# Three projection chunks on rows times scale, shift by one-column products, and earlier operands at three later seams

## The chip, the cores and the metric

The kernel runs on one core of a Trainium2 chip. Five engines work from queues of their own, each in its own order: TensorE (PE, matrix products; its weight loads are listed apart as PEld), VectorE (DVE), ScalarE (ACT), GpSimd (POOL) and SyncE (SP, which here issues the DMA transfers). The metric is the device time of one execution in microseconds (us); lower is better. A run of this kernel has one core and therefore one time.

## The reference

Two layers of a decoder trunk on 1024 tokens of width 1024, batch 1, everything in fp32. Every sub-layer has the same frame:

```python
x = x + gate(c) * rmsnorm_post(f(rmsnorm_pre(x) * (1 + scale(c)) + shift(c)))
# scale, shift, gate: columns of silu(c) @ ada_w + ada_b   (1024 x 6144 weights for each layer)
# layer 0: f = [Mamba-2 SSD heads | MLA heads], read from one projection h @ w_in,
z, xbc, dt_raw, q_a, kv_a, k_pe = split_cols(h @ w_in, L0_SIZES)
xbc = silu(causal_depthwise_conv(xbc, conv_w, conv_b))       # four taps along the tokens
dt  = softplus(dt_raw + dt_bias)
#          then one output projection; then f = SwiGLU FFN with hidden width 2816
# layer 1: f = [GLA heads | NSA heads] in the same way, then its FFN
```

What matters here is the very first product of the program, `h @ w_in` of layer 0 with `h = rmsnorm(x) * gain * (1 + scale) + shift`. With `a = gain * (1 + scale)`, it is also `(rmsnorm(x) * a) @ w_in + shift @ w_in`, and the second term is one number for each column of `w_in`, the same for all tokens. The matrices of scale and shift must be summed from `ada_w` first: eight blocks of 128 rows and 1024 columns (512 KB) each.

## The kernel before

**Products.** An fp32 product is made of three products of a rounded type (`mm3`, L111): each operand is split into a high part (a ScalarE copy, L132 for weights, L144 for activations) and a low part (a subtraction, L133 and L145, mostly on VectorE), and TensorE makes high x high (L114), low x high (L115) and high x low (L116). A *chunk* is 128 columns of `l0_w_in` against all tokens, turned so that columns lie on the partitions. It comes in two *halves* of 512 tokens; a half is 8 blocks of the width times 3 products, 24 products into one PSUM bank. PSUM has the banks `bk` (4), `cx` (2) and `sm` (2). The activations `hT` lie in numbered `slab` tiles, four for each half of the tokens, two with high parts and two with low ones.

**Order.** The functions are written in the order of a list of work, and a scheduler gives each engine its own queue by the priority that follows from it. Transfers are issued by SyncE in the order of its queue, and an issue that must wait holds those behind it.

**The start** (`first_h`, L344). SyncE loads eight `ada_w` blocks for scale, then eight for shift (`aw`, five buffers), with rows of x between them. VectorE multiplies each block by a column of `silu(c)` and accumulates (L369, L371). Eight small products with a vector of ones turn the sum into columns (`ada_cols`, L286). Each of the eight x tiles (128 tokens) is squared and summed on ScalarE (L158), its reciprocal root comes from GpSimd (L151, L152), it is scaled by ScalarE (the first four, L353) or VectorE (the last four, L391), transposed by TensorE (L360) and copied into `xT` (L361). When shift is there, VectorE forms `xT*a + s` (L382), ScalarE takes the high part, and VectorE and GpSimd take turns with the low part.

**The first chunks** (`mixer0_ssd`, L599). Chunk 0 (k_pe and dt), with its chain for dt (L569 to L590: transposes, softplus, a triangular product), runs interleaved with chunks 6 and 7, the first two of twelve chunks `xbc`; then come the other ten, one at a time. A chunk of `xbc` is copied out of its bank by ScalarE, and its four-tap convolution and silu run on VectorE (L639, L641, L558) while TensorE is at the next chunks. Later come `z`, the latent chunks and the scan, whose first product (L751) reads the last convolutions back. Blocks of `ada_w` for the later sub-layers are accumulated beside all this (L276), one step at each `pump`.

**The entry of MLA** (`mixer0_latent`, then `mla`). The latent's last chunks end with `token_sumsq` (L848), 24 one-column products that give sums of squares per token; from them come `rstd` and `rq` (L877, VectorE). `mla` then splits `w_v` (a tile called `qt`, L132 and L133) and makes V.

**The FFN's output** (`ffn_out`) goes through 77 *jobs*. A job has an operand tile of two transfers (L1519, L1520), a high part (L1527) and a low part (L1528), and 12 products. Jobs 0 to 4 are prepared early, while the part before it runs; jobs 5 and up take their tiles from the pool `ab`, which is opened once the part before has closed its own. `front` (L1594) then forms the new x by rows, and in layer 0 also normalises them (L391, VectorE) for layer 1.

## Time and profile before

| | |
|---|---|
| three runs | 3165.64, 3176.91, 3178.05 us; median 3176.91 |
| the profiled execution | 3170.91 us, of which the span from first to last instruction is 3169.2 |
| mean granted TensorE clock in it | 0.982 of full |
| TensorE busy | 3015.1 us, 95% of the span |
| VectorE, ScalarE, GpSimd busy | 2166.4, 1313.2, 716.8 us |
| first product of a chunk | at 59.80 us |
| first product of the FFN's output | at 1264.74 us (layer 0) |

Times in the profile count from the start of the span. A row of the timeline has start, duration, engine (SPq is SyncE's queue), line, operation, output<-input, shape and count; behind it, in square brackets, stands how long the engine was idle before and who released it. A row of the stretches has the stretch, its length, then for PE, PEld, DVE, ACT and POOL the busy time and in brackets the count; then the granted clock of TensorE, the share of time that the DMA engines were busy, and GB/s. L12 is line 12 of the kernel before.

### The profile page before, as it was taken

The page shows a single profiled execution, that of the slowest core. Times are in us where ns is not written, and L with a number is a line of the kernel's source. Part 1 is how long each engine was busy: PE and PEld are TensorE (multiplying, and loading weights), DVE is VectorE, ACT ScalarE, POOL GpSimd, SP SyncE. Part 2 cuts the span into 40 slices and gives each one's busy share as a digit, 9 for nine tenths or more (in the row PEclk, how much of TensorE's full clock was granted, in tenths as well). Part 3 has the DMA queues.
Part 4 walks back from the last instruction along what each step waited for, and adds up shares of the span by engine and source line. Part 5 has one row for each costly group of instructions (what it writes and reads, how often), then busy time and mean ns, then how long its engine had stood idle before and what let it go on. Part 6 is the DMA issues. An engine that isn't in the chain of part 4 may idle for free. (4 is left out here: it accounts for less than half of the span.)

```text
span 3169.2 us, 42961 instructions
## 1 busy us (share of the span) xinstructions
PE 3015.1 (95%) x15832; PEld 2439.2 (77%) x15832; DVE 2166.4 (68%) x3375; ACT 1313.2 (41%) x2159; POOL 716.8 (23%) x678
## 2 busy tenths in 40 slices
PE   5999999999899999999999999889999999999998
PEld 4787777677787888787888888767777787888786
DVE  6667656767887777666737554677766877777655
ACT  4345334545632223445432432355555632223433
POOL 3003334210133223001204423022222114222001
PEclk9999989999999999999999999999999999999999
DMA  6555533324645455984425333331312645455854
GB/s 220 152 187 192 186 99 107 99 73 143 219 156 187 172 202 192 314 281 166 151 93 188 107 120 120 122 107 56 99 49 89 230 165 181 161 207 201 294 195 156
DMA packets 222866, 510.16 MB, mean 161 GB/s; under 512 B 23824, under 2 KB 62832, under 8 KB 221632
## 3 DMA queue, kind: packets, MB, share of 16 engines
q1 hardware_dynamic: 222656, 507.42, 47.0%
q8 instruction: 125, 2.05, 0.3%
q14 instruction: 85, 0.70, 0.1%
HBM read 370.09 MB, written 137.25 MB: 160 GB/s over the span
## 5 line engine op out<-in xcount | busy, mean ns | idle before, releaser
L115 PE MATMUL bk<-slab,whi 128*128 128x512 f32 x1208 | 479.5, 397 | 2.3 <-DVE slab L145 2.3
L114 PE MATMUL bk<-slab,whi 128*128 128x512 f32 x784 | 325.4, 415 | 6.7 <-ACT whi L132 3.5
L116 PE MATMUL bk<-slab,wlo 128*128 128x512 f32 x784 | 311.4, 397 | 2.4 <-DVE wlo L133 2.4
L115 PEld LDWEIGHTS bk<-slab,whi 128*128 128x128 f32 x1208 | 230.4, 191 | 53.3 <-DVE slab L145 3.2
L114 PE MATMUL bk<-T,whi 128*128 128x512 f32 x528 | 210.3, 398 | 2.5 <-DVE blk L1422 2.5
L116 PE MATMUL bk<-T,wlo 128*128 128x512 f32 x528 | 207.8, 394 | 0.0
L151 POOL TENSOR_SCALAR rstd<-ss 128x1 f32<-128x1 f32 (+1 forms) x86 | 31.7, 369 | 713.6 <-ACT junk L158 640.7
L114 PEld LDWEIGHTS bk<-slab,whi 128*128 128x128 f32 x784 | 151.3, 193 | 43.7 <-issue 7.0
L116 PEld LDWEIGHTS bk<-slab,wlo 128*128 128x128 f32 x784 | 150.1, 191 | 35.6 <-DVE wlo L133 2.6
L1218 ACT ACTIVATE whi<-rawa 128x512 fp32r<-128x512 f32 (+1 forms) x108 | 80.6, 749 | 190.0 <-PE bk L115 159.3
L114 PE MATMUL cx<-slab,whi 128*128 128x512 f32 x368 | 146.5, 399 | 6.6 <-ACT blk L1270 5.9
L2172 POOL TENSOR_SCALAR pexp<-pexp,rs 128x640 f32<-128x640 f32 (+7 forms) x128 | 96.3, 756 | 245.6 <-DVE rs L2171 95.2
L115 PE MATMUL cx<-slab,whi 128*128 128x512 f32 x368 | 145.2, 395 | 0.6 <-DVE slab L145 0.6
L116 PE MATMUL cx<-slab,wlo 128*128 128x512 f32 x368 | 145.3, 395 | 0.0
L1004 PE MATMUL sm<-ident,pexp 128*128 128x128 f32 x816 | 132.4, 278 | 6.2 <-POOL pexp L2172 2.3
L1446 POOL TENSOR_TENSOR blk<-blk,blk 128x512 f32<-128x512 f32 x22 | 35.3, 1604 | 423.9 <-DVE blk L1442 327.1
L1004 PEld LDWEIGHTS sm<-ident,pexp 128*128 128x128 f32 x816 | 93.5, 140 | 43.9 <-issue 19.6
L1006 ACT COPY pT<-sm 128x512 f32<-128x512 f32 (+2 forms) x144 | 76.4, 531 | 113.0 <-PE sm L1004 112.4
L1219 DVE TENSOR_TENSOR wlo<-rawa,whi 128x512 fp32r<-128x512 f32 (+1 forms) x108 | 118.2, 1095 | 7.2 <-ACT whi L1218 6.5
L114 PEld LDWEIGHTS bk<-T,whi 128*128 128x128 f32 x528 | 99.0, 188 | 28.1 <-DVE blk L1422 3.3
L276 DVE SCALAR_TENSOR_TENSOR adaacc<-ada,silu_c,adaacc 128x1024 f32<-128x1024 f32 x70 | 100.3, 1432 | 28.8 <-DMA ada<-in_l_ada_w_dram 28.6
L2168 ACT ACTIVATE pexp<-pexp,nm 128x640 f32<-128x640 f32 (+7 forms) x128 | 94.0, 735 | 60.8 <-DVE nm L2166 44.7
(635 smaller groups left out, 8505.9 us busy)
## 6 DMA issues: line engine op xcount, KB each, us to landing
ada<-in_l_ada_w_dram SPq DMA_DIRECT2D x80, 512.0 KB, 4.1
hid<-blk SPq DMA_DIRECT2D x154, 256.0 KB, 2.0
raw<-in_l_w_in_dram SPq DMA_DIRECT2D x51, 512.0 KB, 3.6
ab<-hid SPq DMA_DIRECT2D x96, 256.0 KB, 4.4
cat<-cat SPq DMA_DIRECT2D x64, 256.0 KB, 2.6
ab<-wt SPq DMA_DIRECT2D x60, 256.0 KB, 4.2
raw<-in_l_w_gate_dram SPq DMA_DIRECT2D x28, 512.0 KB, 3.6
raw<-in_l_w_up_dram SPq DMA_DIRECT2D x28, 512.0 KB, 4.5
```

The source lines that it names most:

```text
L114: mm(out, lh, rh, start=start, stop=False, skip_group_check=more)
L115: mm(out, lh, rl, start=False, stop=False, skip_group_check=more)
L116: mm(out, ll, rh, start=False, stop=stop, skip_group_check=more)
L151: nc.gpsimd.tensor_scalar(r, ss, inv_d, EPS, op0=ALU.mult, op1=ALU.add)
L276: ins = nc.vector.scalar_tensor_tensor(acc, r, self.cs[:, k:k + 1], acc, op0=ALU.mult, op1=ALU.add)
L1004: nc.tensor.transpose(ps[:, k * P:(k + 1) * P], e[:, (b + k) * P:(b + k + 1) * P], self.ident)
L1006: (nc.scalar.copy if self.evac else nc.vector.tensor_copy)(pt[:, b:b + m, :], ps[:, :m * P].rearrange("p (k c) -> p k c", c=P))
L1218: nc.scalar.activation(hi, src, AF.Copy)
L1219: (eng or nc.vector).tensor_tensor(lo, src, hi.bitcast(F32), op=ALU.subtract)
L1446: ptt(c, c, state[pm, 0]["u3"], op=ALU.mult)
L2168: nc.scalar.activation(e, e, AF.Exp, bias=nm, scale=-1.0, accum_out=rs)
L2172: nc.gpsimd.tensor_scalar(e, e, rs, 0.0, op0=ALU.mult, op1=ALU.add)
```

## The change

1. `first_h` makes its loads in the order block of scale, row tile of x, block of scale, and so on; blocks of shift come after the four other row tiles. All eight row tiles are now scaled by ScalarE, and their transposes use `sm` banks.
2. Once scale is there, `hT` is filled with `xT*a` without shift (`scaled`: high part on ScalarE with a as its scale, low part on VectorE in one instruction). The three first chunks (0, 6 and 7, whose raw weights stay in memory as `first0` to `first2`) are multiplied with it into six banks that are held until later. The shift blocks are accumulated meanwhile.
3. When shift is there, 24 products with one column each (three chunks times eight blocks, raw weights times s) give three columns `col`, and these are added when the six banks are copied out. `hT` is made a second time, with shift (`shifted`: every second block's sum by ScalarE, all low parts on VectorE, none on GpSimd), for chunk 8 and the following ones. Chunks 8 and 9 run together, half 0 of both first. The chain of dt and the convolutions of chunks 6 and 7 are begun behind that. One `pump` is called for each chunk from 10 on.
4. `w_v` is loaded and split in the latent's last part, ahead of `token_sumsq`, and `rq` moves from VectorE to GpSimd. The buffers of `w_v` later serve the second of two q tiles.
5. In `ffn_out` (both layers) job 5 takes a tile of the pool `rawa`, and the loads of jobs 5 and 6 are issued right behind those of job 4.
6. `front` of layer 0 normalises its rows on ScalarE instead of VectorE (8 instructions).

The core of the diff:

```diff
-    def first_h(self, pool, hT):
+    def first_h(self, pool, keep, hT):
...
+        def scaled(h):
+            for k in range(KD):
+                v, c = xT[h][:, k, :], a[:, k:k + 1]
+                hi, lo = (self.hk(hT, h, p, k, al) for p in range(2))
+                nc.scalar.activation(hi, v, AF.Copy, scale=c)
+                nc.vector.scalar_tensor_tensor(lo, v, c, hi.bitcast(F32), op0=ALU.mult, op1=ALU.subtract)
+
+        def shifted(h):
+            for k in range(KD):
+                v = xT[h][:, k, :]
+                if k % 2:
+                    nc.scalar.activation(v, v, AF.Identity, scale=a[:, k:k + 1], bias=s[:, k:k + 1])
                 else:
+                    nc.vector.tensor_scalar(v, v, a[:, k:k + 1], s[:, k:k + 1], op0=ALU.mult, op1=ALU.add)
+                self.split(self.hk(hT, h, 0, k, al), self.hk(hT, h, 1, k, al), v)
+
+        banks = [[self.cx(), self.cx()], [self.bk(), self.bk()], [self.bk(), self.bk()]]
...
+        for i in range(4):
+            load_a(1, i)
+            load_x(i)
+        load_a(1, 4)
...
+        split_w(0)
+        scaled(0)
+        dense(0, 0)
+        split_w(1)
+        normal(4)
+        normal(5)
+        dense(1, 0)
+        split_w(2)
+        normal(6)
+        normal(7)
+        dense(2, 0)
...
+        steps(0, 4)
+        scaled(1)
+        steps(4, KD)
+        dense(0, 1)
+        later = [self.split_w(self.ring, I["l0_w_in"][8])]
+        s = self.ada_shift(0, 0, self.ada_cols(acc[0]))
+        shifted(0)
+        dense(1, 1)
+        later.append(self.split_w(self.ring, I["l0_w_in"][9]))
+        dense(2, 1)
+
+        ps = self.sm()
+        for n in range(3):
             for k in range(KD):
+                nc.tensor.matmul(ps[:, n:n + 1], raws[n][:, k * P:(k + 1) * P], s[:, k:k + 1], start=(k == 0),
+                                 stop=(k == KD - 1))
+        col = self.t(keep, [P, 3], "col")
+        nc.vector.tensor_copy(col, ps[:, :3])
+        return banks, col, shifted, later
...
-            self.side_by_side(self.chunk("l0_w_in", 0, hT, misc, misc_end, w=self.w0), xbc(0), xbc(1, bank=self.cx))
-            for j in range(2, XBC_N):
-                self.side_by_side(xbc(j))
+            banks, col, shifted, w = first
+            three = [(misc, misc_end), xbc(0), xbc(1)]
+            for n in (1, 2, 0):
+                for h, hs in enumerate(HALVES):
+                    three[n][0](h, hs, banks[n][h])
+            shifted(1)
+            close_first.close()
+            sp = self.pool(e, "ssd")
+            two = [self.chunk("l0_w_in", 6 + j, hT, *xbc(j), w=w[j - 2]) for j in (2, 3)]
+            live = [g for g in two if self.half(g)]
...
+            for _, after in three:
+                after()
+            self.side_by_side(*live)
+            for j in range(4, XBC_N):
+                self.pump()
+                self.side_by_side(self.chunk("l0_w_in", 6 + j, hT, *xbc(j)))
...
+                S["wv"] = self.split_w(keep, I["w_v"], tag="wv", bufs=1)
                 r = self.rstd(self.token_sumsq(sq, self.sm()), NT, 1.0 / 384)
-                nc.vector.tensor_scalar(rq, r, 96 ** -0.5, None, op0=ALU.mult)
+                nc.gpsimd.tensor_scalar(rq, r, 96 ** -0.5, None, op0=ALU.mult)
...
-            if n < 2 or n == 4:
+            if n < 2 or n in (4, 5):
                 return self.t(fw, [P, 1024], "rawa", bufs=4)
...
         for n in range(EARLY):
             prep(n)
+            if n == EARLY - 1:
+                for more in (EARLY, EARLY + 1):
+                    load(more)
             yield
...
-                self.normalise(xt, yi)
+                nc.scalar.activation(yi, xt, AF.Copy, scale=self.rstd(self.sumsq(xt), 1, 1.0 / D))
```

How the queues stand, at three places. **TensorE, from the last row tiles to the first chunk.** Before, all eight row tiles (`xt`) and both sets of columns (L286: scale, then shift) stand ahead of the first product of a chunk:

```order
L286 MATMUL sm_197<-ones_83,acc_29_118 128x1 x8
L360 MATMUL bk_225<-ident_78,xt_216 128x128 x4
L360 MATMUL bk_231<-ident_78,xt_216 128x128 x4
L360 MATMUL bk_255<-ident_78,xt_246 128x128 x4
L360 MATMUL bk_261<-ident_78,xt_246 128x128 x4
L286 MATMUL sm_282<-ones_83,acc_58_209 128x1 x8
L360 MATMUL bk_326<-ident_78,xt_317 128x128 x4
```

After the change four row tiles and scale's columns do:

```order
L368 MATMUL sm_217<-ident_78,xt_140 128x128 x4
L368 MATMUL sm_223<-ident_78,xt_140 128x128 x4
L368 MATMUL sm_238<-ident_78,xt_144 128x128 x4
L368 MATMUL sm_244<-ident_78,xt_144 128x128 x4
L286 MATMUL sm_258<-ones_83,acc_32_123 128x1 x8
L114 MATMUL cx_124<-slab_19_106,whi_286 128x512
L115 MATMUL cx_124<-slab_20_107,whi_286 128x512
```

The other four row tiles' transposes now stand between the products of chunk 6, and shift's columns (L286) behind half 1 of chunk 0. Behind the six halves stand the new one-column products, and then chunk 8:

```order
L467 MATMUL sm_611<-shift_531,first_77_250 128x1 x8
L467 MATMUL sm_611<-shift_531,first_78_252 128x1 x8
L467 MATMUL sm_611<-shift_531,first_83_270 128x1 x8
L114 MATMUL bk_705<-slab_19_106,whi_518 128x512
L115 MATMUL bk_705<-slab_20_107,whi_518 128x512
```

They are 24 more instructions of the program, and there was nothing like them at this place.

**VectorE at the entry of MLA** (`ss` is what `token_sumsq` gives, `qtlo` the low part of `w_v`, `V` the first result). Before:

```order
L851 COPY ss_555_3252<-sm_3227 128x8
L873 SCALAR_TENSOR_TENSOR qlo_2963<-bk_3174,gq_2968,qhi_2962 128x512
L877 TENSOR_SCALAR rq_2964<-rstd_556_3254 128x8
L133 TENSOR_TENSOR qtlo_3308<-raw_3305,qthi_3307 128x1024
L139 SCALAR_TENSOR_TENSOR wa0lo_3339<-raw_3336,wg_3319,wa0hi_3338 128x512 x2
L145 TENSOR_TENSOR catlo_3333<-cat_3322,cathi_3332 128x512
L905 COPY V_3304<-sm_3311 128x512
```

After the change:

```order
L955 COPY ss_567_3337<-sm_3312 128x8
L977 SCALAR_TENSOR_TENSOR qlo_3039<-bk_3250,gq_3044,qhi_3038 128x512
L1011 COPY V_3374<-sm_3375 128x512
L139 SCALAR_TENSOR_TENSOR wa0lo_3403<-raw_3400,wg_3383,wa0hi_3402 128x512 x2
L139 SCALAR_TENSOR_TENSOR wa1lo_3411<-raw_3408,wg_3383,wa1hi_3410 128x512 x2
```

`rq` has left this queue, and the low part of `w_v` (now `wvlo`) stands 25 instructions ahead of `ss`.

**SyncE at the output of layer 0's FFN** (`hid` and `in_l_w_down_dram` or `wt` feed a job's tile). Before, behind job 4's two loads come stores of `wt` and the loads of jobs 2 and 3; job 5's (`ab_10522`) stand 27 instructions further on:

```order
L1519 DMA rawa_10455<-hid_6741 128x512
L1520 DMA rawa_10455<-in_l_w_down_dram 128x512
L1485 DMA wt_6742<-ada_10218 128x1024
L1485 DMA wt_6742<-adaacc_10219 128x1024
L1519 DMA raw_10390<-hid_6741 128x512
```

After the change:

```order
L1628 DMA rawa_10519<-hid_6805 128x512
L1629 DMA rawa_10519<-in_l_w_down_dram 128x512
L1628 DMA rawa_10525<-hid_6805 128x512
L1629 DMA rawa_10525<-in_l_w_down_dram 128x512
L1593 DMA wt_6806<-ada_10282 128x1024
```

The tile `rawa_10525` is job 5's; the tiles `ab` now begin with job 7's.

More of the change, by code (lines that the diff above doesn't have):

```diff
@@ new lines, in first_h, with step, load_w @@
+        acc = [self.t(pool, [P, 1024], f"acc{j}") for j in range(2)]
+        def step(j, i):
+            if i == 0:
+                nc.vector.tensor_scalar(acc[j], aw.pop((j, i)), self.cs[:, 0:1], None, op0=ALU.mult)
+            else:
+                nc.vector.scalar_tensor_tensor(acc[j], aw.pop((j, i)), self.cs[:, i:i + 1], acc[j], op0=ALU.mult,
+                                               op1=ALU.add)
+        raws, w = [], []
+        def load_w(n):
+            raws.append(self.t(keep, [P, 1024], f"first{n}"))
+            nc.sync.dma_start(raws[n], I["l0_w_in"][(0, 6, 7)[n]])
@@ new lines, in split_w @@
+        def split_w(n):
+            hi, lo = (self.t(self.ring, [P, 1024], "w" + p, F32R) for p in ("hi", "lo"))
+            self.split(hi, lo, raws[n])
+            w.append((hi, lo))
+        def scaled(h):
[4 more added lines that the diff above has]
+                nc.vector.scalar_tensor_tensor(lo, v, c, hi.bitcast(F32), op0=ALU.mult, op1=ALU.subtract)
@@ new lines, in dense @@
+        def dense(n, h):
+            for _ in self.dense_t(w[n], hT, h, banks[n][h]):
+                pass
+        for i in range(4):
+            load_a(1, i)
+            load_x(i)
+        load_a(1, 4)
+        self.setup_gains()
+        for i in range(KD):
+            step(1, i)
+            if i + 5 < KD:
+                load_a(1, i + 5)
+            if i % 2:
+                normal(i // 2)
+        for n in range(2):
+            load_w(n)
+        load_x(4)
+        load_x(5)
+        a = self.ada_scale(0, 1, self.ada_cols(acc[1]), self.gains[0, "mix"])
@@ new lines, in first_h, with steps @@
+        load_w(2)
+        load_x(6)
+        load_x(7)
+        for i in range(5):
+            load_a(0, i)
+        split_w(0)
[9 more added lines that the diff above has]
+        dense(2, 0)
+        def steps(n, m):
+            for i in range(n, m):
+                step(0, i)
+                if i + 5 < KD:
+                    load_a(0, i + 5)
+        steps(0, 4)
@@ L597, in dt_chain, with mixer0_ssd @@
                               csT[g::2, :].rearrange("h (c l) -> h c l", l=P))
-    def mixer0_ssd(self, hT, keep):
+    def mixer0_ssd(self, hT, keep, first, close_first):
         nc, I, S = self.nc, self.I, self.S
@@ L643, in after, with each @@
                     self.to_cat(S["xbc"], j, a)
-                return self.chunk("l0_w_in", 6 + j, hT,
-                                  lambda h, hs, ps: nc.scalar.copy(v[:, 3 + h * 512:3 + (h + 1) * 512], ps), after, **kw)
+                def each(h, hs, ps):
+                    o = v[:, 3 + h * 512:3 + (h + 1) * 512]
+                    if j < 2 and h:
+                        nc.vector.tensor_scalar(o, ps, col[:, j + 1:j + 2], None, op0=ALU.add)
+                    elif j < 2:
+                        nc.scalar.activation(o, ps, AF.Identity, bias=col[:, j + 1:j + 2])
+                    else:
+                        nc.scalar.copy(o, ps)
+                return each, after
             def z(j):
@@ L939, in mla_pair @@
             w = self.split_w(pool, I["w_q"][2 * p + j], width=384, tag="wq", bufs=1)
-            th = self.t(pool, [P, T], "qthi", F32R, bufs=2)
-            tl = self.t(pool, [P, T], "qtlo", F32R, bufs=2)
+            home, tag = (S["wvpool"], "wv") if j else (pool, "qt")
+            th = self.t(home, [P, T], tag + "hi", F32R, bufs=1)
+            tl = self.t(home, [P, T], tag + "lo", F32R, bufs=1)
             for h, hs in enumerate(HALVES):
@@ L1513, in raw, with load, prep @@
             return self.t(pools["near"], [P, 1024], "ab", bufs=4)
-        def prep(n):
+        raws = {}
+        def load(n):
             p, pm = jobs[n]
-            r = raw(n)
+            r = raws[n] = raw(n)
             nc.sync.dma_start(r[:, FIRST], hid[HID[p], pm])
             nc.sync.dma_start(r[:, SECOND], source(p, pm))
+        def prep(n):
+            if n not in raws:
+                load(n)
+            r = raws.pop(n)
             k = n % NS
```

65 lines of the change are left out of this document (24 added, 41 removed).

## The prediction

> **What bounds the kernel now.** I read the busy shares first, then the stretches of the start, then the waits of TensorE and the timeline around each. TensorE is busy for 95% of the span:
>
> ```profile
> PE 3015.1 (95%) x15832; PEld 2439.2 (77%) x15832; DVE 2166.4 (68%) x3375; ACT 1313.2 (41%) x2159; POOL 716.8 (23%) x678
> ```
>
> So only time in which TensorE idles or runs at a lower clock can be won, 154 us of idling at most, unless its work shrinks. The change adds to its work. The largest hole is the start. Columns behind the length: busy time of PE, PEld, DVE, ACT, POOL, then the clock, DMA share and GB/s.
>
> ```profile
> 0.00:20.00 20.00, 1.97 (x8) 1.57 (x8) 10.36 (x12) 6.44 (x10) 6.27 (x16) 1.00 0.85 304
> 20.00:40.00 20.00, 11.18 (x50) 10.30 (x50) 9.99 (x10) 9.78 (x14) 3.40 (x4) 1.00 0.94 339
> 40.00:60.00 20.00, 8.79 (x41) 8.07 (x41) 17.19 (x21) 13.72 (x24) 12.76 (x12) 1.00 0.35 123
> 80.00:100.00 20.00, 16.27 (x75) 12.15 (x74) 9.67 (x15) 5.91 (x8) 0.00 (x0) 0.94 0.52 172
> ```
>
> For 40 us the transfers set the pace (share 0.85 and 0.94), then VectorE does (17.19 of 20). The chunks' products run from here to here:
>
> ```profile
> 14.92 3.92 DVE L371 SCALAR_TENSOR_TENSOR acc<-aw,silu_c,acc 128x1024 f32<-128x1024 f32 x3 [1.21 <-DMA aw<-in_l_ada_w_dram]
> 37.93 3.57 PE L286 MATMUL sm<-ones,acc 128*128 128x1 f32 x16 [0.70 <-DVE acc L371]
> 59.80 0.62 PE L114 MATMUL bk<-slab,whi 128*128 128x512 f32 x1
> 65.49 0.39 PE L114 MATMUL bk<-slab,whi 128*128 128x512 f32 x1
> 70.93 0.39 PE L114 MATMUL cx<-slab,whi 128*128 128x512 f32 x1
> 86.85 0.42 PE L569 MATMUL sm<-ident,ca 16*128 16x16 f32 x4 [1.34 <-DVE ca L626]
> 96.90 0.49 PE L582 MATMUL sm<-dtx,triu 128*128 128x128 f32 x2 [2.39 <-DVE dtx L580]
> 100.27 0.63 PE L114 MATMUL bk<-slab,whi 128*128 128x512 f32 x1
> 100.69 0.79 DVE L639 TENSOR_SCALAR ca<-cv,cw,cb 128x1024 f32<-128x1024 f32 x1
> 122.45 0.39 PE L114 MATMUL bk<-slab,whi 128*128 128x512 f32 x1
> ```
>
> A half takes 5.44 us at the full clock (65.49 to 70.93). Six halves and the dt chain end at 100.27; chunks 8 and 9 end at 122.45, where chunk 10 starts. That instant is my mark for the start.
>
> **The start, step by step.** Scale's sum is ready at 18.84 (14.92 + 3.92) with two row tiles loaded between its blocks; now there are four. Two more 512 KB at the 339 GB/s of the row above are 3.1 us: about 22. ScalarE paces the row tiles (square, scale, two copies):
>
> ```profile
> 8.44 1.06 ACT L158 ACTIVATE junk<-xt 128x1024 bf16<-128x1024 f32 x1 [5.63 <-DMA xt<-in_x_dram]
> 24.26 1.06 ACT L158 ACTIVATE junk<-xt 128x1024 bf16<-128x1024 f32 x1 [0.90 <-DMA xt<-in_x_dram]
> 26.36 1.15 ACT L353 ACTIVATE xt<-xt,rstd 128x1024 f32<-128x1024 f32 x1 [0.94 <-POOL rstd L152]
> 29.56 0.59 ACT L361 COPY xT<-bk 128x512 f32<-128x512 f32 x1 [0.27 <-PE bk L360]
> ```
>
> That is 3.6 us a tile (the square's second, short instruction not counted), and with its idling some 4.1 when tiles overlap; four from 8.44 on end near 25. Scale's columns (3.57 in the row at 37.93) follow, then the first slab: the first product at 29.5 instead of 59.80, 30.3 us earlier. What it costs to get there:
> - TensorE starts cold. Its ramp is priced below at 2.2 us. Half 0 of chunk 0 ends near 37.
> - Half 0 of chunks 6 and 7 (10.9) with four row tiles between, paced by ScalarE's 4.1 us a tile: near 53.5. Half 1 of chunk 0: 58.9. Shift's columns: 61 (2 us warm). Two more halves: 71.9.
> - The 24 one-column products are 48 instructions. Their nearest rows are MLA's:
>
> ```profile
> 428.95 3.18 PE L848 MATMUL sm<-ones,sq 128*128 128x1 f32 x28
> 435.25 4.41 PE L848 MATMUL sm<-ones,sq 128*128 128x1 f32 x20
> 428.00:436.00 8.00, 8.00 (x53) 7.80 (x51) 0.33 (x2) 3.34 (x5) 0.00 (x0) 0.76 0.40 120
> 444.00:452.00 8.00, 7.66 (x25) 6.11 (x25) 4.78 (x8) 1.69 (x4) 2.01 (x3) 0.67 0.74 230
> ```
>
> The first 28 take 0.114 us each, the next 0.22, because the granted clock halves although TensorE was never idle in that stretch (8.00 of 8.00). So 28 x 0.114 + 20 x 0.22 = 7.6 us (10.6 if all are slow, 5.5 if none is), and after them the dense products stay at half rate for some 4.5 us, a loss of 2.2 (8 us at 0.67 in the last row, less the part of it that TensorE waits).
> - `col` and copying out the bank that chunk 8 wants: two instructions and their hand-overs, 1.2. That makes 80.7.
> - Chunks 8 and 9: 4 x 5.44 = 21.8, plus 2.2 for the clock, plus the dt chain with its stalls and its slow clock as before, 100.27 - 59.80 - 6 x 5.44 = 7.8: 112.5.
>
> 112.5 against 122.45 gives **10 us gained**; 4 if ScalarE's row tiles come 6 us later (another 1.5 each), 14 if the one-column products don't slow the clock.
>
> The Trainium skill ("TensorE: Matmul & The Clock Gate", "What's actually happening") says that the clock halves after an idle window of about 3.4 us and comes back after one of sustained work. By it the 24 products, issued without a pause, would keep the full clock and cost 5.5 with no ramp, and the gain would be 14. The stretch from 428 on has no idling and a clock of 0.76; I go by it.
>
> **Cover.** Making `hT` twice costs ScalarE and VectorE 16 more high and low parts. It is hidden while TensorE does two halves and the one-column products (60 to 80). VectorE has 16 low parts, eight sums and two low parts of weights from 61 on. The latter are 1.21 each (the row of `qtlo` below); a low part is 0.68, and a sum, on the same width, no longer: 19 us, ready near 80 to 88 with waits; chunk 8's half 1 needs it near 94. Without that cover the excess counts fully. What is late next is VectorE's convolutions: they began at 100.69 with chunk 10 at 122.45, and now begin near 105 with chunk 10 at 112.5. That is a backlog of some 14 us, which has to be gone when the scan reads them, where there is no slack now:
>
> ```profile
> 43.86 0.68 DVE L145 TENSOR_TENSOR slab<-xT,slab 128x512 fp32r<-128x512 f32 x1
> 122.00:232.00 110.00, 110.00 (x483) 90.40 (x482) 76.73 (x69) 48.42 (x83) 3.58 (x7) 1.00 0.49 155
> 235.19 0.71 PE L751 MATMUL cx<-bc 128*128 128x128 f32 x4 [0.65 <-DMA bc<-xbc]
> ```
>
> VectorE idles 33 us of the 110 in the second row, so the backlog vanishes; the term is nothing, and 1 us per us beyond 33.
>
> **MLA's entry.** The wait to be removed:
>
> ```profile
> 439.69 0.17 DVE L851 COPY ss<-sm 128x8 f32<-128x8 f32 x1 [3.90 <-PE sm L848]
> 441.93 1.23 DVE L877 TENSOR_SCALAR rq<-rstd 128x8 f32<-128x8 f32 x1 [1.42 <-POOL rstd L152]
> 443.07 1.21 DVE L133 TENSOR_TENSOR qtlo<-raw,qthi 128x1024 fp32r<-128x1024 f32 x1
> 444.34 0.80 PE L115 MATMUL sm<-qtlo,kvhi 128*128 128x512 f32 x1 [3.63 <-DVE qtlo L133]
> ```
>
> VectorE's queue holds `qtlo` behind `rq`, which waits for GpSimd. With the low part made 25 instructions earlier and `rq` on GpSimd, TensorE goes on: 3.6 us, and a little of the slow clock behind it. V is then done sooner, and the next operands (rope, keys) may be waited for instead: **-4**, between -2 and -5. The split itself (1.06 and 1.21) moves beside dense chunks and costs nothing there.
>
> **The FFN's seams.** Job 5's tile is loaded too late, in both layers:
>
> ```profile
> 1239.42 0.43 SPq L1520 DMA_DIRECT2D rawa<-in_l_w_down_dram  x1
> 1274.61 0.43 SPq L1520 DMA_DIRECT2D ab<-in_l_w_down_dram  x1
> 1280.81 1.06 ACT L1527 ACTIVATE slab<-ab 128x1024 fp32r<-128x1024 f32 x1 [7.68 <-DMA ab<-in_l_w_down_dram]
> 1281.91 1.09 PE L114 MATMUL sm<-slab 128*128 128x512 f32 x2 [3.37 <-ACT slab L1527]
> 1268.00:1278.00 10.00, 10.00 (x46) 8.28 (x45) 6.45 (x9) 2.01 (x2) 0.00 (x0) 1.00 0.96 341
> 1282.00:1286.00 4.00, 4.00 (x11) 2.87 (x12) 2.35 (x2) 1.06 (x1) 0.00 (x0) 0.57 0.92 310
> 2958.01 1.22 PE L114 MATMUL sm<-slab 128*128 128x512 f32 x2 [3.86 <-ACT slab L1527]
> ```
>
> The idling is 3.37 and 3.86 us, and behind each the clock of 0.57 over 4 us loses 1.7: 10.6 in all. Job 5's load now stands behind job 4's at 1239.4. What is late next is job 7, which takes the first `ab` tile: ready near 1280.81 + 1.06 and a low part of 1.21, at 1283.1, wanted after seven jobs of 2.72 us from 1264.74, at 1283.8. The margin is 0.7 us and the transfers are nearly full (0.96), so I take **-10.5**, at worst -5 (job 7 waits some 2 us in each layer and the clock drops again).
>
> **Between the layers** eight instructions of 0.75 us leave VectorE, and eight of 1.15 (the row at 26.36) come to ScalarE:
>
> ```profile
> 1482.10 0.75 DVE L391 TENSOR_SCALAR y<-xt,rstd 128x1024 f32<-128x1024 f32 x1 [0.39 <-POOL rstd L152]
> 1510.00:1520.00 10.00, 6.22 (x34) 5.01 (x33) 8.38 (x14) 7.21 (x16) 0.00 (x0) 0.88 0.13 42
> 1519.30 0.80 PE L114 MATMUL bk<-slab,whi 128*128 128x512 f32 x1 [2.96 <-ACT slab L144]
> ```
>
> VectorE is the fuller engine (8.38 against 7.21), but the last wait is for ScalarE. Bounds -4 (6 us off VectorE, part on the path) and +1 (0.4 us for each of the last tiles); I take **-1.5**, nearer to nothing since both engines are full.
>
> **Sum.** -10 - 4 - 10.5 - 1.5 = -26. The profiled execution took 3170.91 us, 3169.2 of span, 6.0 below the median of 3176.91; the middle of the four times is near 3173, so its 3145 becomes **3147**, 0.9% below the median. This kernel's measurements tell 0.5%, 15.9 us, from no change.
>
> **Rivals.**
> - *The start gives nothing* (0.20). The extra 16 high and low parts, the held banks and the cold clock eat the lead: if ScalarE, with eight row tiles, eight scaled blocks and two weights for half 1, ends at 63 instead of 53, all 10 us are gone. For it: ScalarE's idling between square and scale (0.94 in its row); against it: ScalarE has some 21 us of such work between 30 and 54 (four tiles at 3.6, eight blocks and two weights). 3173 - 16 = 3157. That the early chunks don't do what they should, because scale's loads are later than 22, ends here too.
> - *The seam's stall only moves* (0.09): job 7 instead of job 5, or keys instead of `qtlo`: -10 - 5 - 2 - 1.5: 3155.
> - *The clock stays full through one-column products* (0.06): -30, 3143. It has only the skill's rule for it.
> - *Slower: VectorE's backlog reaches the scan* (0.05). VectorE works in order; a dt instruction waiting for TensorE's transposes, now behind both half-0s, stops the convolutions and copies behind it. The scan's first product then waits us for us beyond 33 of backlog, and past 33 + 26 = 59 the change loses. With convolutions from 167 instead of 105 the backlog is 76, and the time 3173 - 26 + 43 = 3190. Against it: the dt chain took 10 us before (86.85 to 96.90).
> - The forecast has the remaining 0.60.
>
> **Range.** The forecast's own bounds are -34 (14 + 5 + 10.6 + 4) and -10 (4 + 2 + 5 less 1); the first three rivals lie inside or near. With part of the 6 us by which runs differ from their middle: 3134 to 3167. Faster by over 0.5% means under 3161: nearly all of the forecast and of the clock's rival, most of the moved stall's and half of the first rival's, 0.72; within it 0.22; slower 0.06.
>
> **What would show it.** Right: the first chunk's product near 29.5, the one-column products near 72 with a clock under 1 behind them, chunk 10 near 112.5, the scan's first product near 225 without a long wait; no wait of over a us for `qtlo`'s successor near 432 or for a job's slab near 1260. Wrong: chunk 10 after 118, a wait at the scan's first product over 3 us, a new wait for job 7, or TensorE waiting more between the layers than before.

## The result, and the profile after

| | before | after |
|---|---|---|
| runs | 3178.05, 3176.91, 3165.64, 3175.03 | 3150.23, 3152.10, 3144.50, 3147.72 |
| median | 3175.97 us | 3148.97 us |
| profiled execution | 3170.91 (span 3169.2) | 3150.23 (span 3148.5) |

The ratio is 0.9921, with the interval 0.9907 to 0.9936: faster by 0.8%. The forecast was 3147, with 3134 to 3167 as its range. The total is right, but of its four terms only the first brings what was forecast, and more; the other three brought less than half, nothing, or a loss. This is what the next parts show.

The busy shares of the kernel after:

```profile
PE 3025.7 (96%) x15880; PEld 2449.0 (78%) x15880; DVE 2160.0 (69%) x3381; ACT 1340.6 (43%) x2193; POOL 695.3 (22%) x671
```

TensorE has 48 instructions more (the one-column products) and is busy for 10.6 us longer, in a span that is 20.7 us shorter. So idling fell by some 31 us. Its timeline at the start, with line numbers of the kernel after (L114 to L116 are the chunks' products as before, L467 the one-column products, L653 to L673 the dt chain, L855 the scan's first product):

```profile
30.37 0.80 PE L114 MATMUL cx<-slab,whi 128*128 128x512 f32 x1 [1.27 <-ACT slab L396]
60.48 1.84 PE L286 MATMUL sm<-ones,acc 128*128 128x1 f32 x16
72.93 5.96 PE L467 MATMUL sm<-shift,first 128*128 128x1 f32 x48
79.86 0.79 PE L114 MATMUL bk<-slab,whi 128*128 128x512 f32 x1 [0.97 <-ACT cv L731]
93.09 0.66 PE L653 MATMUL sm<-ident,ca 16*128 16x16 f32 x8
98.15 0.38 PE L666 MATMUL sm<-dtx,triu 128*128 128x128 f32 x2
99.07 1.04 PE L673 MATMUL sm<-ident,cs 128*16 128x128 f32 x8
105.89 0.39 PE L114 MATMUL bk<-slab,whi 128*128 128x512 f32 x1
218.54 0.71 PE L855 MATMUL cx<-bc 128*128 128x128 f32 x4 [0.58 <-DMA bc<-xbc]
```

The first chunk's product stands at 30.37 instead of 59.80, and chunk 10 at 105.89 instead of 122.45. The columns of the stretches are those of the prediction's:

```profile
20.00:40.00 20.00, 16.37 (x59) 13.33 (x58) 12.86 (x17) 14.93 (x23) 1.72 (x4) 1.00 0.88 343
40.00:60.00 20.00, 19.30 (x101) 15.78 (x100) 13.66 (x15) 14.51 (x23) 5.13 (x10) 1.00 0.49 161
76.00:79.00 3.00, 2.89 (x22) 2.80 (x21) 0.07 (x1) 0.00 (x0) 0.00 (x0) 0.77 0.00 0
79.00:82.00 3.00, 2.14 (x5) 1.75 (x6) 2.97 (x6) 2.88 (x6) 0.00 (x0) 0.50 0.00 0
82.00:85.00 3.00, 3.00 (x9) 2.33 (x9) 2.97 (x6) 2.63 (x6) 0.00 (x0) 0.59 0.40 87
85.00:88.00 3.00, 3.00 (x14) 2.47 (x14) 3.00 (x8) 1.79 (x4) 0.00 (x0) 1.00 0.00 0
```

TensorE is busy for 16.37 and 19.30 of 20 us between 20 and 60, where it was for 11.18 and 8.79. The last four rows are the price: a clock of 0.77, 0.50 and 0.59 from the one-column products on, and 1.00 again in the last.

**Where the time came from.** The start of the same instruction in both profiles, and their difference, is the lead of the kernel after. It changes in few places:

| place | before | after | lead | change |
|---|---|---|---|---|
| chunk 10 | 122.45 | 105.89 | 16.6 | +16.6 |
| scan's first product | 235.19 | 218.54 | 16.65 | 0 |
| the scan, some 19 us on | 254.09 | 233.47 | 20.6 | +4 |
| first product of layer 0's FFN output | 1264.74 | 1241.57 | 23.2 | +2.6 |
| its job 6; its job 30 | | | 28.5; 23.35 | +5.3; -5.2 |
| first chunk of layer 1 | 1519.30 | 1500.78 | 18.5 | -5 |
| first product of layer 1's FFN output | 2940.35 | 2922.28 | 18.1 | -0.4 |
| its job 6; the last product | | | 23.9; 18.5 | +5.8; -5.4 |
| end of the span | 3169.2 | 3148.5 | 20.7 | +2.2 |

In this pair the first stage and the scan bring 20.6 us, the whole gain. One pair of profiles carries some error at this scale: one kernel (that of experiment 2) profiled twice led by 17.8 and by 27.2 at the first product of layer 0's FFN output, and the kernel after, profiled again, led by 20.3 behind the scan, 22.4 before and 26.35 behind layer 0's FFN seam, and 27.6 at the end. A stage is therefore believed below only where several kernels show it.

### The profile page after: what moved, and what is told of

The parts are those of the page before. It is cut to its first block, busy times and chain, and to the rows that moved or that the text cites. A ratio compares the mean times of both kernels' runs of the same rounds, so it can differ in the third digit from the quotient of the medians.

```text
span 3148.5 us, 43054 instructions
## 1 busy us (share of the span) xinstructions
PE 3025.7 (96%) x15880; PEld 2449.0 (78%) x15880; DVE 2160.0 (69%) x3381; ACT 1340.6 (43%) x2193; POOL 695.3 (22%) x671
## 5 line engine op out<-in xcount | busy, mean ns | idle before, releaser
L114 PE MATMUL bk<-slab,whi 128*128 128x512 f32 x784 | 327.7, 418 | 6.9 <-ACT whi L132 3.4
L116 PE MATMUL bk<-slab,wlo 128*128 128x512 f32 x784 | 314.3, 401 | 2.4 <-DVE wlo L133 2.4
L114 PE MATMUL bk<-T,whi 128*128 128x512 f32 x528 | 210.3, 398 | 1.1 <-DVE blk L1530 1.1
L116 PE MATMUL bk<-T,wlo 128*128 128x512 f32 x528 | 207.8, 393 | 0.0
L114 PEld LDWEIGHTS bk<-slab,whi 128*128 128x128 f32 x784 | 152.6, 195 | 43.9 <-issue 7.0
L116 PEld LDWEIGHTS bk<-slab,wlo 128*128 128x128 f32 x784 | 151.6, 193 | 36.0 <-DVE wlo L133 2.6
L1326 ACT ACTIVATE whi<-rawa 128x512 fp32r<-128x512 f32 (+1 forms) x108 | 80.7, 750 | 196.3 <-PE bk L115 156.9
L114 PE MATMUL cx<-slab,whi 128*128 128x512 f32 x368 | 148.5, 405 | 8.3 <-ACT blk L1378 5.9
L116 PE MATMUL cx<-slab,wlo 128*128 128x512 f32 x368 | 146.2, 397 | 0.0
L114 PEld LDWEIGHTS bk<-T,whi 128*128 128x128 f32 x528 | 99.3, 188 | 26.7 <-DVE blk L1530 1.6
L116 PEld LDWEIGHTS bk<-T,wlo 128*128 128x128 f32 x528 | 99.2, 188 | 24.4
```

The lines of the kernel that those rows point to most:

```text
L114: mm(out, lh, rh, start=start, stop=False, skip_group_check=more)
L116: mm(out, ll, rh, start=False, stop=stop, skip_group_check=more)
L1326: nc.scalar.activation(hi, src, AF.Copy)
```

## The experiments

Kernels measured in one series ran on the same chip, against the same runs of the kernel before.

**1. The start alone, and everything but the start.** The first kernel has parts 1 to 3 of the change, the second parts 4 to 6 (its `first_h` and `mixer0_ssd` are those of the kernel before).

```diff
 the start alone:
-                S["wv"] = self.split_w(keep, I["w_v"], tag="wv", bufs=1)
-                nc.gpsimd.tensor_scalar(rq, r, 96 ** -0.5, None, op0=ALU.mult)
+                nc.vector.tensor_scalar(rq, r, 96 ** -0.5, None, op0=ALU.mult)
...
-            if n < 2 or n in (4, 5):
+            if n < 2 or n == 4:
...
-                nc.scalar.activation(yi, xt, AF.Copy, scale=self.rstd(self.sumsq(xt), 1, 1.0 / D))
+                self.normalise(xt, yi)
```

> The first three parts of the change alone (the start); MLA's entry, both FFN seams and the layer seam are as before. Theory now (the trace after shows chunk 10 at 105.89 instead of 122.45, and another 4 us won in the scan's first 20 us): this part alone brings some 20 us, so the time is the changed kernel's within 3 us, near 3149 to 3152 against 3176 before. Rival (the prediction's terms): the start brings 10, so about 3166.

> The start as before; w_v split early and rq on GpSimd, the early loads at the FFN seams and the ScalarE normalisation between the layers as changed. Theory now: +2.5 from MLA's entry, about 0.5 in each FFN seam (won at job 5, given back by job 30), -6 between the layers: no change within 3 us, about 3178. Rival (the prediction's terms -4, -10.5, -1.5): 16 us faster, about 3160.

The start alone took 3146.16 us, ratio 0.9926 (0.9913 to 0.9938); the rest alone 3173.92, ratio 1.0011 (1.0002 to 1.0020). The start's interval covers the full change, and the other three parts together, on the old start, gain nothing. The wait for job 5 is still in the start's profile (line numbers 4 less than after):

```profile
1258.47 1.22 PE L114 MATMUL sm<-slab 128*128 128x512 f32 x2 [3.30 <-ACT slab L1638]
```

In the rest's profile that wait is gone, and its lead rises from 0.2 to 5.6 us at job 6. At job 12 it is -2.0, behind this wait, and between the layers it falls by another 5:

```profile
1299.33 0.77 PE L114 MATMUL sm<-slab 128*128 128x512 f32 x1 [3.65 <-DVE uacc L1594]
```

**2. The normalising of rows back on VectorE**, the rest as changed. It ran twice, the second time beside the changed kernel.

```diff
-                nc.scalar.activation(yi, xt, AF.Copy, scale=self.rstd(self.sumsq(xt), 1, 1.0 / D))
+                self.normalise(xt, yi)
```

> The changed kernel with the eight normalisations between the layers back on VectorE. Theory: they made ScalarE late for the next layer's operands, so 4 to 6 us faster than the changed kernel, near 3144, with the lead over before at the first chunk of layer 1 near 23 us instead of 18. Rival: the loss there comes from something else that stands a few us differently (order of jobs, adaLN steps), and the time stays at 3149 within 2 us.

> The kernel with the normalisations on VectorE once more, on the chip of the run beside it, so that the two can be told apart: if its ratio to before is again 0.991, the 0.13% by which it stood below the changed kernel's ratio is its own; if it is 0.992 or more, the two differ by less than the chips do.

> The changed kernel itself, unaltered, on the same chip. Theory: slower than the kernel with the normalisations on VectorE by the 4 to 5 us that the layer seam loses, about 0.14%. Rival: within 1 us of it, the loss at the seam being made up in layer 1.

3141.68 us (0.9908, interval 0.9895 to 0.9922) in the first series; in the second 3139.38 (0.9911, interval 0.9894 to 0.9927) beside 3144.52 (0.9925, interval 0.9910 to 0.9940) for the changed kernel. The ratios' intervals overlap, so the 5 us between them are not settled by the times. The stage is: from job 30 of layer 0's FFN to the first chunk of layer 1, every profiled kernel with the normalising on ScalarE lost 4.8 to 5.3 us against the kernel before (after, its repeat, the rest alone, and experiments 3, 5 and 7), and every one with it on VectorE 0.5 at most (both of these, the start alone, and those of experiments 4 and 6). The stretches of the seam, aligned by the same instruction, first of the kernel after, then of the second run with VectorE:

```profile
1441.50:1456.50 15.00, 13.34 (x69) 10.70 (x68) 7.54 (x10) 11.24 (x21) 2.95 (x8) 1.00 0.57 191
1456.50:1476.50 20.00, 14.06 (x62) 10.12 (x61) 15.04 (x20) 13.24 (x25) 4.02 (x10) 0.93 0.38 133
1476.50:1501.50 25.00, 20.96 (x96) 16.98 (x96) 15.84 (x21) 18.73 (x35) 3.28 (x11) 0.91 0.25 81
```

```profile
1437.80:1452.80 15.00, 13.49 (x68) 10.52 (x66) 10.39 (x13) 9.52 (x20) 3.27 (x8) 1.00 0.50 177
1452.80:1472.80 20.00, 16.59 (x76) 12.47 (x77) 17.81 (x25) 13.44 (x30) 5.26 (x12) 1.00 0.45 159
1472.80:1492.80 20.00, 15.83 (x82) 12.68 (x81) 15.11 (x22) 11.94 (x25) 2.58 (x8) 1.00 0.22 75
```

The work takes 60 us instead of 55. VectorE is relieved (38.4 against 43.3 us in the three rows), ScalarE pays (43.2 against 34.9), and TensorE does the less in the middle row, 14.06 against 16.59. Its waits there in the kernel after (`hv`: a normalised and transposed tile with scale and shift applied, L495 the half by ScalarE, L498 the half by VectorE):

```profile
1455.17 0.66 PE L484 MATMUL sm<-ident,y 128*128 128x128 f32 x4 [1.47 <-ACT hv L495]
1471.73 0.66 PE L484 MATMUL sm<-ident,y 128*128 128x128 f32 x4 [2.81 <-ACT hv L495]
1500.78 0.65 PE L114 MATMUL bk<-slab,whi 128*128 128x512 f32 x1 [2.58 <-ACT slab L144]
```

The 2.81 us is new. Of every tile ScalarE already makes the `hv` of one half, a square and a high part; the eight instructions of 1.15 us stand in the same queue ahead of them.

**3. Without the early loads of jobs 5 and 6**, the rest as changed.

```diff
-            if n < 2 or n in (4, 5):
+            if n < 2 or n == 4:
...
-            if n == EARLY - 1:
-                for more in (EARLY, EARLY + 1):
-                    load(more)
```

> The changed kernel without the early loads of jobs 5 and 6. Theory: the transfers are what is late at the seam, the stall comes back at job 5 (3.4 and 3.9 us with the slow clock behind it) and the waits at jobs 7, 8, 11 and 28 shrink; in all the same time within 2 us. Rival: the early loads are worth 5 us in each layer, and other things cost them later: 8 to 10 us slower.

3149.07 us, ratio 0.9937 (0.9923 to 0.9950). Job 5 waits again:

```profile
1259.88 0.73 PE L114 MATMUL sm<-slab 128*128 128x512 f32 x2 [2.36 <-ACT slab L1642]
```

And yet the lead passes the seam of layer 0 from 21.0 to 21.9 us: with job 5 stalled, little further on is late. With the early loads the lead rises by 5.3 there and then falls by 5.2. In layer 1 the seam costs 2.3 us without them, and with them it brings 0.4.

The other profiles show how far this varies. All ten kernels profiled with the early loads win some 5.3 us up to job 6 in layer 0 and 5.8 in layer 1; by job 30 they have given back 0.9 to 7.5 and 3.9 to 6.9. The two seams together then stand between 3.4 us lost and 5.7 won, on average 2 won; in the repeat of the kernel after it is 5.2. The two kernels without the loads lose 1.4 (this one) and 4.0 (the start alone). So by the stages the loads are worth some 4 to 5 us against the same kernel without them, with a spread as large; by the times up to 5 (0.9937 against 0.9921 and 0.9925, intervals that overlap).

**4. What takes the gain back.** The first wait behind the early jobs in the kernel after is for a copy that VectorE makes of a finished sum (`uacc`, L1698), whose bank job 11's products want. VectorE's queue just ahead (L1643 is the low part of a later job's tile; between the rows shown stands a step of a later adaLN matrix):

```profile
1268.60 1.22 DVE L1643 TENSOR_TENSOR slab<-ab,slab 128x1024 fp32r<-128x1024 f32 x1 [2.76 <-ACT slab L1642]
...
1270.06 1.23 DVE L1643 TENSOR_TENSOR slab<-ab,slab 128x1024 fp32r<-128x1024 f32 x1 [0.24 <-ACT slab L1642]
...
1271.86 1.21 DVE L1643 TENSOR_TENSOR slab<-ab,slab 128x1024 fp32r<-128x1024 f32 x1
1273.00 0.68 DVE L1698 COPY uacc<-sm 128x512 f32<-128x512 f32 x1
```

```profile
1273.83 0.47 PE L114 MATMUL sm<-slab 128*128 128x512 f32 x1 [2.08 <-DVE uacc L1698]
```

VectorE stood idle for 2.76 us on a tile that had not come, then had three low parts and another step to do before the copy. This place takes 2.4 of the 5.2 us. The other 2.7 go at one later place, which the repeat doesn't have: TensorE waits for the last step of a later adaLN matrix (L276) and makes its columns (L286), and the clock falls behind them.

```profile
1321.59 1.92 PE L286 MATMUL sm<-ones,adaacc 128*128 128x1 f32 x16 [0.89 <-DVE adaacc L276]
1323.50:1326.90 3.40, 3.40 (x10) 2.62 (x10) 3.22 (x4) 2.11 (x2) 0.00 (x0) 0.50 1.06 397
```

The edits that follow are about the first place. Two theories: the order on VectorE costs the time (then fewer low parts ahead of the copy keep the gain), or the transfers do, and the copy is only where it shows. The first edit leaves out the preparing of tiles at the last two jobs of the first run of eleven jobs, on top of experiment 2:

```diff
-                advance()
+                if p != "1" or pm < NM - 2:
+                    advance()
```

> The changed kernel with the normalisations back on VectorE, and in the FFN's first run (jobs 0 to 10) the preparation of two more operand tiles moved behind the four copies of the sums. Theory: at job 11 TensorE waits 1.7 to 3.7 us because the copies stand in VectorE's queue behind low parts whose loads are late; with these two behind the copies that wait falls under 0.7 us in both layers, and with the slow clock behind it 3 to 5 us are won against the kernel with the normalisations on VectorE alone. Rival: the transfers are what is late, so the wait moves to a later job's operand, and at most 1 us is won.

3140.23 us, ratio 0.9906 (0.9891 to 0.9921), like experiment 2. The scheduler put the same 15 low parts ahead of the first copy as without the edit, so the edit decides nothing between the theories. But with these 15 ahead, layer 0's wait at job 11 was 2.08, 1.00, 1.75, 3.22 and 0.49 us in five profiles (the kernel after, its repeat, both of experiment 2, and this one), so the order alone doesn't set it. The second edit holds the low parts of jobs 12 to 17 behind the copies and leaves the loads where they are:

```diff
-            tt(lo, r, hi.bitcast(F32), op=ALU.subtract)
+            ins = tt(lo, r, hi.bitcast(F32), op=ALU.subtract)
+            if 12 <= n < 18:
+                self.pin(ins)
...
-                advance()
+                if p != "1" or pm < 2:
+                    advance()
+                elif NS - 1 + pm < 18:
+                    load(NS - 1 + pm)
```

> The changed kernel with the normalisations on VectorE, and at the FFN's seams the low parts of jobs 12 to 17 held behind VectorE's copies of the first run's sums, while their loads are issued as before: 12 low parts stand ahead of the first copy instead of 15 (the earlier attempt to move two preparations left 15 there, so it moved nothing that matters). Theory: what makes job 11 wait is that the copies stand in VectorE's order behind low parts whose loads are late; the wait there (1.75 and 1.95 us with the normalisations on VectorE alone) falls under 0.5 in both layers, and with the slow clock behind it 4 to 8 us are won in all. Rival: the transfers themselves are short, so the time comes back as waits for the operands of jobs 12 to 20, and less than 1 us is won.

3140.44 us, ratio 0.9910 (0.9894 to 0.9927), against 3139.38 without the edit on the same chip. Twelve low parts stand ahead now, job 11 no longer waits, but job 12 does, and the lead falls by 3.6 us; in layer 1 it falls from 29.1 to 25.2 behind two waits at earlier jobs:

```profile
1277.11 0.69 PE L114 MATMUL cx<-slab 128*128 128x512 f32 x1 [1.94 <-DVE uacc L1703]
2937.14 0.49 PE L114 MATMUL sm<-x 128*128 128x512 f32 x1 [0.87 <-ACT x L1642]
2938.40 0.50 PE L115 MATMUL sm<-x 128*128 128x512 f32 x1 [0.76 <-DVE x L1643]
```

The order on VectorE decides which job waits; how much is lost stays within what the other profiles lose. That speaks for the transfers, and the stretch in layer 1 of the kernel after agrees, with a DMA share of 0.97 over 40 us:

```profile
2930.00:2970.00 40.00, 37.14 (x154) 29.52 (x153) 27.34 (x28) 20.00 (x20) 0.00 (x0) 0.96 0.97 340
```

In layer 0 the share of 1265 to 1275 is 0.83, so there it is less certain: what was late is a tile's load, and no run showed it come sooner. That the transfers are the cause is therefore argued, not shown.

**5. Without the one-column products** (the first three chunks then lack the term of shift).

```diff
-        for n in range(3):
-            for k in range(KD):
-                nc.tensor.matmul(ps[:, n:n + 1], raws[n][:, k * P:(k + 1) * P], s[:, k:k + 1], start=(k == 0),
-                                 stop=(k == KD - 1))
...
-        nc.vector.tensor_copy(col, ps[:, :3])
+        nc.vector.tensor_copy(col, s[:, :3])
```

> The changed kernel without the 24 one-column products: the three columns come from other numbers, so shift's share of the three first chunks is left out. Theory: chunk 8 then starts near 73.5 instead of 79.86 and at the full clock (the products cost 5.96, their hand-over 0.97 and the half clock behind them 2.2), chunk 10 near 97 instead of 105.89. Rival: the clock's fall comes from something else at this place, or the slabs with shift are not ready: chunk 8 after 76, or a clock under 0.9 in 76 to 84 all the same.

One execution: 3145.47. Chunk 8 starts at 71.90, 8.0 us before that of the kernel after, and chunk 10 at 95.75, 10.1 before. The clock stays full:

```profile
79.00:88.00 9.00, 9.00 (x46) 7.07 (x44) 7.12 (x16) 4.22 (x8) 0.00 (x0) 1.00 0.37 119
```

Of the 10.1, the products are 5.96 and their hand-over to chunk 8 another 0.97. By 1.0 this execution was ahead already at shift's columns (59.45 against 60.48). The remaining 2.2 is between chunk 8 and chunk 10: the slowed clock, on products that are not the cause of it. The nine profiles with this start and all 48 instructions in one row have chunk 10 at 105.1 to 107.1, so the 10.1 is good to a us or so.

**6. The one-column products in two groups** (two chunks' after the fifth half, the third chunk's after the sixth), on top of the first edit of experiment 4, to keep each group below the length that slows the clock.

```diff
+        def columns(n):
+            for k in range(KD):
+                nc.tensor.matmul(ps[:, n:n + 1], raws[n][:, k * P:(k + 1) * P], s[:, k:k + 1], start=(k == 0),
+                                 stop=(k == KD - 1))
+
         dense(1, 1)
+        columns(0)
+        columns(1)
         later.append(self.split_w(self.ring, I["l0_w_in"][9]))
         dense(2, 1)
+        columns(2)
```

> As the kernel with the normalisations on VectorE and the copies ahead, and the one-column products no longer in one block: 16 behind half 1 of chunk 6, 8 behind half 1 of chunk 7. Theory (the clock falls for a long row of one-column products, not for a short one): full clock at chunk 8, so chunk 10 some 2 us earlier than in the changed kernel, and the whole 2 us faster than the kernel without this step. Rival: the clock falls all the same, and nothing is won.

3142.31 us, ratio 0.9910 (0.9896 to 0.9924); chunk 10 at 105.18, 0.7 earlier than in the kernel after and within the 105.1 to 107.1 of the nine profiles. Its two groups, and stretches from the first group on:

```profile
66.25 3.65 PE L464 MATMUL sm<-shift,first 128*128 128x1 f32 x32
76.89 1.84 PE L464 MATMUL sm<-shift,first 128*128 128x1 f32 x16
79.70 0.58 PE L114 MATMUL bk<-slab,whi 128*128 128x512 f32 x1 [0.97 <-ACT cv L735]
```

```profile
68.00:71.00 3.00, 3.00 (x20) 2.81 (x21) 2.76 (x4) 1.36 (x2) 0.00 (x0) 0.79 0.00 0
71.00:74.00 3.00, 3.00 (x10) 2.35 (x10) 1.61 (x3) 2.57 (x5) 0.00 (x0) 0.64 0.60 175
74.00:77.00 3.00, 3.00 (x16) 2.49 (x15) 0.00 (x0) 1.05 (x2) 0.00 (x0) 1.00 0.00 0
...
80.00:83.00 3.00, 3.00 (x8) 2.30 (x7) 2.94 (x6) 3.00 (x6) 0.00 (x0) 0.50 0.18 41
```

Both groups slow the clock: 32 instructions over 3.65 us, and 16 over 1.84 us with the wait of 0.97 behind them. The ramp is paid twice, and what the faster products win is lost again.

**7. Without the added `pump` of each chunk from 10 on.** It was to test whether that step brings the 4 us at the scan.

```diff
-                self.pump()
```

> The changed kernel without its one additional step of the later adaLN matrices for each chunk from 10 on. Theory: these steps had left the scan's entry, where they stood before VectorE's operands for GpSimd; without the additional steps two or three of them stand there again, TensorE waits 1 to 2 us for xdd, and of the 4 us won between the scan's first product and 20 us later 2 to 4 are lost. Rival: that gain comes from elsewhere (the convolutions' backlog, GpSimd's faster instruction); it stays.

One execution: 3174.3, as slow as the kernel before (3169.5 in this series). The gain at the scan stays (its lead goes from 18.2 to 22.3 there), so that theory fell. But at the end of the latent part the last adaLN matrix is not done (L276 on VectorE is one of its eight steps, L286 on TensorE its columns):

```profile
449.06 1.28 DVE L276 SCALAR_TENSOR_TENSOR adaacc<-ada,silu_c,adaacc 128x1024 f32<-128x1024 f32 x1 [3.76 <-DMA ada<-in_l_ada_w_dram]
```

```profile
450.49 3.54 PE L286 MATMUL sm<-ones,adaacc 128*128 128x1 f32 x16 [35.92 <-DVE adaacc L276]
```

TensorE stands for 35.92 us. The lead of 23 becomes -14.4 behind it, and -4.4 by layer 0's FFN output. The new start takes away places at which these steps used to be called; without the added `pump` its gain is lost, 25 to 30 us by the times (3174.3 against 3148.97 and 3144.52 in other series).

## Why the prediction was right, and where it was wrong

**The start: the mechanism right, -10 was -16.6** (15.3 to 17.3 in the nine profiles with this start). The instants were foreseen closely: first product 29.5 (measured 30.37), one-column products from 71.9 (72.93), chunk 8 at 80.7 (79.86). The mis-sized term is "the dt chain with its stalls and its slow clock as before ... 7.8". Chunks 8 and 9 took 26.0 us (79.86 to 105.89); 21.8 is their four halves and some 2.1 the clock, which leaves 2.1 for the chain. Its products (L653, L666, L673 above) follow the dense ones without a wait, because two chunks' halves now lie around them; before, they waited 1.34 and 2.39 us with little to cover them. That the convolutions' backlog would vanish held: VectorE's first one stands in the last row here, 5 us before chunk 10 instead of 22, and the scan's first product waits 0.58, as before (0.65).

```profile
100.92 0.80 DVE L720 TENSOR_SCALAR ca<-cv,cw,cb 128x1024 f32<-128x1024 f32 x1
```

**The one-column products: 7.6 was 5.96, the clock's price of 2.2 was 2.2.** The nine profiles have 5.93 to 8.09, so the products vary around the forecast. The longest is in the first run of experiment 2:

```profile
72.53 8.09 PE L467 MATMUL sm<-shift,first 128*128 128x1 f32 x48
75.00:80.00 5.00, 5.00 (x25) 5.00 (x25) 0.00 (x0) 0.00 (x0) 0.00 (x0) 0.50 0.00 0
```

There the clock is at half by 75, some 2.4 us into the row; in the kernel after it is 1.00 up to 77.60, 4.7 us in. Where the clock falls sets what the products cost.

The rival of a full clock fell. The rows tell it first: TensorE idles nowhere in 76 to 79 (2.89 of 3.00, the rest the step to the next row), the clock is 0.77 there and 0.50 in the next stretch, and in experiment 5, without these products, it is 1.00. The Trainium skill ("TensorE: Matmul & The Clock Gate", "What's actually happening") has the clock halve after an idle window of about 3.4 us. In the row of 48 TensorE did not idle at all, and in experiment 6 sixteen such instructions with a wait behind them, 2.81 us together, were enough; by the rows such products act like idling, which the section does not say, and so short a stretch does not agree with its length.

**MLA's entry: -4 was nothing.** The 3.63 us are gone, and the lead rises by 2.5 us from `token_sumsq` to this place (22.4 to 24.9; the clock falls 1 us sooner among the one-column products than before, which takes 1.6 of the gain). Behind it the rest is lost to waits that grew, as "the next operands (rope, keys) may be waited for instead" had it: for V (0.76 and 0.78, before 0.33), `ss` (1.06, before 0.54) and the second q tile (1.06, before 0.81). The wait for the keys is not new (1.97, before 2.10). Two of them:

```profile
432.95 0.50 PE L114 MATMUL sm<-wvhi,kvhi 128*128 128x512 f32 x1 [0.78 <-DVE V L1011]
441.87 1.12 PE L1021 MATMUL sm<-qv,Rep 64*128 64x512 f32 x2 [1.06 <-DVE ss L1169]
```

From 429 to 510 the lead changes by +0.1 in the kernel after and by -0.8 to +2.1 in the nine other profiles that have this part and get through this stage (all but experiment 7), on average by +0.4. This part was not tried by itself; a us or two stays open.

**The FFN's seams: -10.5 was -0.6 in this pair, -5.2 in the repeat and -2 on average.** The step "job 5's tile is loaded too late" was right in mechanism and size: the lead rises by 5.3 and 5.8 us, 5.1 and 5.6 by the prediction's rows. What failed is "what is late next is job 7 ... the margin is 0.7 us". Not one job was late but a row of tiles behind it, and time came back at jobs 7 to 12, in layer 1 in every profile with the loads; the later wait for adaLN columns took as much again in layer 0 of this one (experiments 3 and 4). The rival "the stall only moves" was the right one here; it left 5 of the 10.5 standing, more than the average. The row that spoke for it was quoted: a DMA share of 0.96 around the stall. That the removed stall had given the transfers time to catch up fits experiment 3 and is not shown by itself.

**Between the layers: -1.5 was +5.** This step failed in its sign. "Nearer to nothing since both engines are full" went by the busy shares of one stretch. The wait that ended last there (2.96 us, for ScalarE) was quoted beside it and named the engine that could bear no more. The bound of +1 counted only the last tiles; eight instructions of 1.15 us in ScalarE's queue delayed `hv` in the middle of the seam too (2.81), and the clock was lower with the longer waits (0.93 and 0.91 in the rows of experiment 2, against 1.00).

**Not foreseen: 4 us at the scan.** This wait of the kernel before is gone (L789 on GpSimd makes `xdd` from VectorE's `xd`, L783):

```profile
238.83 1.28 DVE L276 SCALAR_TENSOR_TENSOR adaacc<-ada,silu_c,adaacc 128x1024 f32<-128x1024 f32 x1 [2.47 <-DMA ada<-in_l_ada_w_dram]
...
243.44 0.69 DVE L783 TENSOR_TENSOR xd<-sm,dt 128x512 f32<-128x512 f32 x1
...
244.80 2.87 POOL L789 TENSOR_TENSOR xdd<-xd,dec 128x1024 f32<-128x1024 f32 x1 [59.14 <-DVE xd L783]
247.73 1.98 PE L820 MATMUL sm<-xdd,bn 128*128 128x512 f32 x2 [2.01 <-POOL xdd L789]
```

The wait is 2.01 us, and the clock of 0.50 in the stretch from 248 to 250 behind it makes the rest of the 4. A step of a later adaLN matrix waited 2.47 us for its load with `xd` queued behind it. In the kernel after no such step stands there: `xd` comes 4.5 us after the scan's first product (223.04) instead of 8.25. Experiment 7 shows that it is not the added `pump` that does it; the steps' place in the new order does, which is read from the two traces and not tried alone. Also not costed: that the added `pump` carries 25 to 30 us (experiment 7).

**The sum.** The terms came out as -16.6, 0, -0.6 and +5, with -4 at the scan and some -4.5 in smaller shifts and the end of the span: -20.7 in the profiled pair. In the repeat of the kernel after it is -27.6 against the same profile, with -5.2 at the FFN. Between the medians it is -27.0, and in the later series -25.1 (3169.63 to 3144.52); the forecast was -26. The profiled execution of before lies 5 us under its median and that of after 1 us above, which makes the 6 us between the first pair and the medians. So the total came out right by errors that cancel, which is luck: in the first pair MLA, the FFN and the layer seam gave 20.4 us less than forecast, the start and the scan 10.6 more (in the repeat some 16 less and 10 more), and the rest lies in shifts that a pair of profiles can't assign. The version that is best by its stages has the whole change except the normalising, which stays on VectorE (0.9908 and 0.9911).

## What to carry to other kernels

A gain at the start of the program, where TensorE idles with nothing to do, stays; a stall removed where transfers are nearly full can come back some jobs later, in part or whole, so size it at the next place that is fed late, not at the wait. Before an instruction is moved to another engine, look whom the last wait of that stage names: the busy shares may favour an engine that ends the stage. And count what the removed code called on the side, since a step of later work without its place turns into a wait that nothing covers.

## What the runs showed of the hardware

Products with one column, issued without a pause, lowered TensorE's granted clock as idling does: 48 instructions over 5.96 us (0.77, then 0.50), 32 over 3.65 us (0.79 and 0.64 in the stretches from 68 to 74), and 16 over 1.84 us followed by a wait of 0.97 us (0.50). The first cost the dense products behind it 2.2 us. Splitting them won nothing at this size. Sixteen alone did not lower it: behind shift's columns (1.84 us at 60.48, no wait) the clock of the kernel after stays at 1.00.

```profile
60.00:72.00 12.00, 12.00 (x62) 10.23 (x61) 10.41 (x19) 10.50 (x17) 0.00 (x0) 1.00 0.29 89
```

Nor is the number of instructions a fixed limit. In the kernel before, two groups of 32 over 3.63 us in layer 1 (L848, at 1682.86 and 1783.61, TensorE busy throughout) were followed by a clock of 1.00 and of 0.50.

The first GpSimd instruction of its kind in the scan, a product of two tiles of 128x1024, took 2.87 us before (L789 above) and 1.90 us after:

```profile
224.40 1.90 POOL L893 TENSOR_TENSOR xdd<-xd,dec 128x1024 f32<-128x1024 f32 x1 [51.73 <-DVE xd L887]
```

In the first, VectorE's next step over 128x1024 (L276) had begun at 244.64 and ran beside it. That alone is not the reason: of the seven such instructions of the kernel after, those at 298.21 and 319.31 had a VectorE step of that width beside them for 1.5 us or more and took 1.91 and 1.90, while the one at 336.50 took 2.79. In both slow ones an L276 step was already running when GpSimd began; why it matters stays open.
